# One late weight slot loaded by a half-width transfer and eight transfers of eight partitions, another slot loaded by rows, and the sums of the last but one expert moved behind the last product

## The chip, the cores and the metric

The kernel runs on one core of one Trainium2 chip. The metric is the device time of one execution in microseconds (us), and three runs of the kernel before give 1457.04 us as their median (1456.44 to 1457.23). One more execution was taken by the hardware profiler; all rows below are from that one.

TensorE (PE in the profile) multiplies matrices and writes to PSUM; VectorE (DVE) and ScalarE (ACT) work on whole tiles; SyncE (SP) issues nearly all the transfers from memory. A transfer is carried by sixteen DMA engines.

## The reference

One block over 256 latent tokens and 256 context tokens: modulated norm, an input projection, retention and latent attention, a merge, and then a layer of 32 experts of which each token takes four. The change lies in the experts, whose core is this (cut):

```python
def moe(h, router_w, router_b, w_gu, b_gu, w_down, b_down):
    logits = tok @ router_w + router_b
    top_val, top_idx = lax.top_k(logits, TOP_K)
    gates = jax.nn.softmax(top_val.astype(jnp.float32), axis=-1)
    ...
    def expert_block(args):
        xb, e = args
        gu = xb @ w_gu[e] + b_gu[e]
        gate, up = gu[:, :D_FF_EXPERT], gu[:, D_FF_EXPERT:]
        gate = jnp.minimum(gate, SWIGLU_LIMIT)
        up = jnp.clip(up, -SWIGLU_LIMIT, SWIGLU_LIMIT)
        glu = gate * jax.nn.sigmoid(SWIGLU_ALPHA * gate)
        return ((up + 1.0) * glu) @ w_down[e] + b_down[e]
    ...
    out = jnp.zeros_like(tok).at[sorted_tok].add(ys[dest] * sorted_gate[:, None].astype(ys.dtype))
```

After it come the residual and a last RMSNorm over each token's 1024 columns. All is float32. An expert has 8 MB of weights for gate and up (1024 x 2048) and 4 MB for down (1024 x 1024), so the 32 experts read 384 MB.

## The kernel before

The experts are done one after the other, each for up to 64 tokens. Their weights come in slots of 2 MB: 128 partitions of 16 KB. An expert takes four slots for gate and up (`load_gu`, line 1171) and two for down (`load_down`, line 1176). There are eleven slots in a ring, and the list `todo` sets the order in which they are filled. For experts 0 to 29 it is four gate/up slots, two down slots, and so on. The last two, 30 and 31, stand together: four slots of 30, four of 31, two down slots of 30, two of 31. The last three of these down slots are loaded by `down_in_parts` (line 1184): four transfers of 512 KB, each a quarter of every partition's 16 KB, so that TensorE can begin on a quarter.

SP issues the transfers in order. Besides the slot, a transfer needs a semaphore that counts its landing. There are eight of them (DMAHW0 to DMAHW7 in the lists below), handed out in turn, and an issue waits until the transfer eight places ahead of it has landed on all its engines.

TensorE's order is written by hand. For each expert `gate_up` (matmuls on line 1539) takes four slots of two k each; in its middle `combine` (line 1525) adds the weighted outputs of the expert before to the sums `total`. `slot_rows` (1512, 1514) makes the rows and gates for that. Then `down` (1572) multiplies by the down slots, and `weigh` scales the result (DVE, 1581) and splits it into a high half on ACT (292) and a low half on DVE (293). These halves live in the tiles `up` and `ga` of a pool with one buffer for each name.

At the end this differs. Expert 30's down products are held back. Its hidden rows are made inside expert 31's `gate_up` (`middle`, line 144 transposes, with the final gain on lines 1590 and 1643). After expert 31's `slot_rows` there are sixteen small matmuls on ones that keep TensorE going (`keep_warm`, line 486), as there are for expert 30. Then come expert 30's down products (1572), expert 31's from its first down slot (1723), the sums of expert 30 (1525), expert 31's from its second down slot (1723), the weighing, and expert 31's sums (`add_product`, 1712). What follows is the last norm (1627 to 1738 on ACT and DVE) and four stores.

Of the kernel before, what the change touches and what calls it, by code (L numbers as in the profile page):

```python
# [25 lines left out]
E = 32  # L26
# [33 lines left out]
def hybrid_block(ctx: ExitStack, tc: tile.TileContext, A, out, dbg=None):  # L60
    nc = tc.nc
# [56 lines left out]
    for i, n in enumerate(("ret_decay_fwd", "ret_decay_bwd")):  # L118
        src = A[n]
# [182 lines left out]
    def bank(*names, shape=(128, 512)):  # L302
        for n in names:
            B[n] = pt_(shape)
# [178 lines left out]
    def keep_warm(n):  # L483

        for _ in range(n):
            nc.tensor.matmul(B["spare"][:, :128], ones, ones, start=True, stop=True)
# [682 lines left out]
    def load_gu(wgu, j):  # L1169
        w = wtile()  # L1170
        nc.sync.dma_start(w, wgu[256 * j:256 * j + 256].rearrange("(p r) n -> p (r n)", r=2))
        return w

    def load_down(wdn, j):
        w = wtile()
        nc.sync.dma_start(w, wdn[512 * j:512 * j + 512].rearrange("(p r) n -> p (r n)", r=4))
        return w

    def down_in_parts(wdn, j):
# [3 lines left out]
        for r in range(4):  # L1183
# [4 lines left out]

    todo = [(f, A[name][0, e], i) for es in [[e] for e in range(E - 2)] + [[E - 2, E - 1]]
            for f, name, n in ((load_gu, "exp_w_gu", 4), (load_down, "exp_w_down", 2)) for e in es for i in range(n)]  # L1190
    todo[-3:] = [(down_in_parts, src, i) for f, src, i in todo[-3:]]

    def fetch():
        f, src, i = todo.pop(0)
# [2 lines left out]
    def take(f, src, i):  # L1197

        if src is not None:
            return f(src, i)  # L1200
        if not fetched:
            fetch()
        return fetched.pop(0)
# [3 lines left out]
    def wtile():  # L1207
        r = slots[nring[0] % len(slots)]
        nring[0] += 1
        return r.tile([128, 4096], F32, name="w")  # L1210
# [153 lines left out]
    def one_hot(oh, pos, ne):  # L1364

        shp = [128, 2, ne, CAP]
        nc.vector.tensor_tensor(oh[:, :, :ne], pos[:, :, :, None].to_broadcast(shp),
                                slot[:, None, None, :].to_broadcast(shp), op=OP.is_equal)
# [33 lines left out]
    def row_of(e):  # L1402
        return lambda q: ident[:, 32 * q + e:32 * q + e + 1]
# [38 lines left out]
    def oh_tile():  # L1442
        return late.tile([128, 2, EG, CAP], F32R, name="oh", bufs=2)
# [57 lines left out]
    def xg_tile():  # L1501
        return late.tile([128, 4, EG * CAP], F32, name="xg", bufs=3)

    def slot_rows(oh, i, g, name="ct"):

        ct = late.tile([128, T], F32R, name=name)
        gs = late.tile([128, 1], F32, name=name + "g")
        ps = pt_()
        for t in range(2):
            for h in range(2):  # L1510
                o = oh[:, t, i].bitcast(F32)
                nc.tensor.matmul(ps[64 * h:64 * h + 64, 128 * t:128 * t + 128], o, ident,
                                 start=(t == 0), stop=True, skip_group_check=True)
                nc.tensor.matmul(ps[64 * h:64 * h + 64, T:T + 1], o, g[:, t], start=False, stop=(t == 1),
                                 skip_group_check=True)
        nc.scalar.activation(ct, ps[:, :T], AF.Copy)
        nc.vector.tensor_copy(gs, ps[:, T:T + 1])  # L1517
        return ct, gs

    def combine(ys, ct, n=CAP, first=False):  # L1520

        for t in range(2):
            for part in ys:
                for h in range(2):
                    nc.tensor.matmul(total[t][h], ct[64 * h:64 * h + n, 128 * t:128 * t + 128],  # L1525
                                     part[64 * h:64 * h + n], start=first, stop=(part is ys[-1]), skip_group_check=True)

    def gate_up(wgu, halves, xg, i, mid=None, ga=None):

        sl = slice(CAP * i, CAP * i + CAP)  # L1530
        g_, u_ = halves[0][0], halves[2][0]
        for k in range(KD):
            if mid and k == MID:
                mid()
            if k % 2 == 0:
                w = take(load_gu, wgu, k // 2)
            for ps, h, c in halves:
                c += 2048 * (k % 2)
                nc.tensor.matmul(ps[64 * h:64 * h + 64], xg[k // 4][:, k % 4, sl], w[:, c:c + 512],  # L1539
                                 start=False, stop=(k == KD - 1), skip_group_check=True)  # L1540
        ga = ga() if ga else xp.tile([128, 512], F32, name="ga")
        up = xp.tile([128, 512], F32, name="up")
        nc.vector.tensor_scalar(ga, g_, LIMIT, None, op0=OP.min)  # L1543
        nc.scalar.activation(g_, ga, AF.Tanh, scale=0.5 * ALPHA)  # L1544
        nc.vector.tensor_scalar(up, u_, LIMIT, -LIMIT, op0=OP.min, op1=OP.max)
        nc.vector.scalar_tensor_tensor(up, up, 1.0, ga, op0=OP.add, op1=OP.mult)
        nc.vector.scalar_tensor_tensor(up, g_, 1.0, up, op0=OP.add, op1=OP.mult)
        return up

    def hidden(up, mid=None, hT=None):  # L1550
        ps = pt_((128, 4, 128))

        fours = up.rearrange("s (p r) -> s r p", r=4)
        for c in range(4):
            transpose(ps[:, c], fours[:, c])
        if mid:
            mid()
        hT = hT() if hT else xp.tile([128, 4, 128], F32, name="ga")
        nc.scalar.activation(hT, ps, AF.Copy, scale=0.5)  # L1559
        return [hT[:, f % 4, 64 * (f // 4):64 * (f // 4) + 64] for f in range(KD)]  # L1560
# [39 lines left out]
    for h in range(2):  # L1600
        r = slice(64 * h, 64 * h + E)
# [9 lines left out]
    def gate_rows():  # L1611
        ps = pt_()
        for t in range(2):
            transpose(ps[:, 128 * t:128 * t + 128], gate[:, t].rearrange("p a s -> p (a s)"))
        nc.scalar.activation(gT, ps[:, :T], AF.Copy)
    def add_tokens(t, h):
        hs = slice(512 * h, 512 * h + 512)
        nc.tensor.matmul(total[t][h], ident, x[:, t, hs], start=False, stop=True, skip_group_check=True)
# [19 lines left out]
    def wide():  # L1638

        w = wtile()  # L1640
        fg = [w[:, 2048 + 512 * h:2560 + 512 * h] for h in range(2)]
        for f, ps in zip(fg, final_gain()):
            nc.scalar.activation(f, ps, AF.Copy)
        return w[:, :2048].rearrange("p (t n) -> p t n", t=2), fg
# [7 lines left out]
    pending, before_last = None, {}  # L1652
    for e in range(E):
        g, i = divmod(e, EG)
        last = e == E - 1

        def middle():
            if e == 0:
                gate_rows()
            elif last:  # L1660
                before_last["hT"] = hidden(before_last["up"])
                before_last["out"] = wide()
            else:
                combine(*pending)
        up = gate_up(None, begun.pop(), xg, i, middle, flat if last else None)
        if E - 8 <= e < E - 4:
            add_tokens(*divmod(e - E + 8, 2))
        if e == 0:
            combine((bdn,), gT, E, True)
        ct, gs = slot_rows(oh, i, gt1[:, :, e:e + 1], "ct2" if last else "ct")  # L1670
        if e >= E - 2:
            bank("spare")
            keep_warm(CLK[8])
        if last:
            break
        if i == 0:
            if g + 1 < E // EG:
                ohn = oh_tile()
                one_hot(ohn, posm[:, :, EG * g + EG:EG * g + 2 * EG], EG)
                xgn = []  # L1680
                rbn = slot_scale(ohn, EG)

        def gather_next():
            if g + 1 < E // EG:
                xgn.append(xg_tile())
                gather(ohn, rbn, xgn[i], i, EG)

        if e:
            gather_next()
        if e == E - 2:  # L1690
            before_last.update(up=up, ct=ct, gs=gs)
            begun.append(gu_bias(row_of(e + 1)))
            continue
        ys = down(None, up, gs, lambda: begun.append(gu_bias(row_of(e + 1))))
        pending = (ys, ct)
        if e == 0:
            gather_next()
        if i == EG - 1 and g + 1 < E // EG:
            oh, xg = ohn, xgn
# [4 lines left out]
    ys = down(None, None, before_last["gs"], None, before_last["hT"], lambda: later.append(hidden(up, None, xg_tile)))  # L1704
# [12 lines left out]
    for j in range(2):  # L1717
        w = take(load_down, None, j)
        for f in range(4 * j, 4 * j + 4):
            for c in range(2):  # L1720
                for h in range(2):
                    o = 1024 * (f % 4) + 512 * h + 256 * c
                    nc.tensor.matmul(pys[c][64 * h:64 * h + 64], hT[f], w[:, o:o + 256],  # L1723
                                     start=(f == 0), stop=(f == KD - 1))
        if j == 0:
            combine(ys, before_last["ct"])
    ys = weigh([(slice(256 * c, 256 * c + 256), pys[c]) for c in range(2)], gs)
    for c in range(2):
        add_product(c)
# [75 lines left out]
```

## Time and profile before

| | |
|---|---|
| median of three runs | 1457.04 us |
| profiled execution, own time | 1458.6 us |
| its span | 1456.8 us |
| TensorE busy | 1406.9 us (97%) |
| from about 540 us on: DMA | about 427 GB/s |

Times are in us from the span's start, mean durations of groups in ns. In rows of the timeline, "0.44 PE L1512 ... x4" is a run of four instructions that together took 0.44 us; what follows in brackets is idle time and who ended it. The share of the span in the chain is the work that ended last, followed back from the last instruction. The profiled execution took 1458.6 us, that is 1.8 us above its span and 1.6 us above the median of the runs.

### The profile page before, as it was taken

The numbers are of one execution on the slowest core, as the hardware profiler recorded it, in microseconds if no ns is written. First come the engines' busy times: TensorE is split into PE (matmuls) and PEld (weight loads), VectorE is DVE, ScalarE is ACT, GpSimd is POOL, SyncE is SP. The second block draws the span as 40 slices with busy tenths as digits, with TensorE's granted clock in tenths as the row PEclk, the third lists the DMA queues.
The fourth block names the chain that finished last, engine by engine and source line by source line (L and its number), as shares of the span: only waits on it lengthen the run. The fifth ranks groups of instructions, "written<-read, shape, count | busy, mean of one in ns | idle before, by whom it ended". The sixth has DMA issues, their size and how long they took to land.

```text
span 1456.8 us, 19073 instructions
## 1 busy us (share of the span) xinstructions
PE 1406.9 (97%) x7973; PEld 814.0 (56%) x7973; DVE 561.8 (39%) x1024; ACT 346.5 (24%) x601; POOL 73.1 (5%) x84
## 2 busy tenths in 40 slices
PE   8999999999999999999999999999999899999996
PEld 6788888888888764444434434434433343334333
DVE  4587866868676642221221221221221121212113
ACT  4455633544443421101100100100100010001101
POOL 3200050110101000000000000000000000000000
PEclk9999999999999999999999999999999999999998
DMA  8733283554558889999999999999999999999995
GB/s 280 231 113 130 73 275 101 188 174 163 183 205 318 312 354 413 423 428 426 427 427 427 426 427 426 428 426 427 426 426 428 425 429 425 428 426 426 426 426 197
DMA packets 79284, 492.39 MB, mean 338 GB/s; under 512 B 6819, under 2 KB 25324, under 8 KB 55000
## 3 DMA queue, kind: packets, MB, share of 16 engines
q1 hardware_dynamic: 78216, 489.22, 83.3%
q0 software_dynamic: 576, 1.23, 0.3%
q8 instruction: 64, 1.05, 0.3%
q10 hardware_dynamic: 400, 0.66, 0.1%
q14 instruction: 28, 0.23, 0.0%
HBM read 490.03 MB, written 1.05 MB: 337 GB/s over the span
## 4 chain that ended last, share of the span: by engine, by line
PE 68%; DMA 25%; DVE 4%; ACT 1%; issue 1%; SPq 0%; POOL 0%; DVEq 0%; ACTq 0%; POOLq 0%
PE gu L1539 19%; DMA w<-in_exp_w_gu_dram 16%; PE ps L1572 9%; PE ps L298 9%; PE ps L296 9%; PE ps L297 9%; DMA w<-in_exp_w_down_dram 8%; PE ps L1488 3%; PE gu L1398 3%; PE ps L144 3%; PE sum L1525 2%; DMA w<-in_ada_w_dram 1%; DVE ws L288 1%; PE ps L330 1%; PE gu L1723 0%
## 5 line engine op out<-in xcount | busy, mean ns | idle before, releaser
L1539 PE MATMUL gu<-w,xg 128*64 128x512 f32 x2048 | 455.8, 595 | 17.7 <-DMA w<-in_exp_w_gu_dram 17.2
L1539 PEld LDWEIGHTS gu<-w,xg 128*64 128x64 f32 x2048 | 142.5, 137 | 307.8 <-issue 266.0
L1572 PE MATMUL ps<-w,ga 128*64 128x512 f32 x992 | 218.4, 592 | 0.0
L1543 DVE TENSOR_SCALAR ga<-gu 128x512 f32<-128x512 f32 x31 | 21.4, 692 | 394.9 <-PE gu L1539 394.9
L288 DVE TENSOR_TENSOR ws<-w,ws 128x1024 fp32r<-128x1024 f32 (+1 forms) x114 | 139.6, 1232 | 43.2 <-ACT ws L287 41.4
L1572 PEld LDWEIGHTS ps<-w,ga 128*64 128x64 f32 x992 | 71.1, 137 | 140.7 <-issue 139.3
L287 ACT ACTIVATE ws<-w 128x1024 fp32r<-128x1024 f32 (+1 forms) x114 | 116.7, 1028 | 73.3 <-PE ps L298 71.0
L1544 ACT ACTIVATE gu<-ga 128x512 f32<-128x512 f32 x31 | 18.7, 602 | 433.0 <-DVE ga L1543 433.0
L1581 DVE SCALAR_TENSOR_TENSOR ps<-ps,ctg,gate 128x512 f32<-128x512 f32 x31 | 23.5, 758 | 245.9 <-PE ps L1572 245.9
L296 PE MATMUL ps<-ws,hh 128*128 128x512 f32 (+3 forms) x304 | 111.7, 367 | 1.1 <-ACT hh L408 1.1
L298 PE MATMUL ps<-ws,hl 128*128 128x512 f32 (+3 forms) x304 | 110.0, 362 | 1.2 <-DVE hl L410 1.2
L297 PE MATMUL ps<-ws,hh 128*128 128x512 f32 (+3 forms) x304 | 110.0, 362 | 0.5 <-DVE ws L288 0.5
L292 ACT ACTIVATE up<-ps 128x512 fp32r<-128x512 f32 x31 | 18.5, 597 | 247.8 <-DVE ps L1581 247.8
L1488 PE MATMUL ps<-oh,x 128*128 128x128 f32 x512 | 68.5, 287 | 4.2 <-DVE ctg L1517 4.0
L1488 PEld LDWEIGHTS ps<-oh,x 128*128 128x128 f32 x512 | 62.7, 196 | 7.2 <-DVE ctg L1517 6.2
L296 PEld LDWEIGHTS ps<-ws,hh 128*128 128x128 f32 x304 | 57.5, 189 | 14.9 <-issue 4.2
L298 PEld LDWEIGHTS ps<-ws,hl 128*128 128x128 f32 x304 | 57.6, 190 | 10.6 <-DVE hl L410 2.2
L297 PEld LDWEIGHTS ps<-ws,hh 128*128 128x128 f32 x304 | 57.6, 189 | 9.8 <-DVE ws L288 1.2
L1398 PE MATMUL gu<-bgu,ident 128*64 128x512 f32 x256 | 62.0, 605 | 0.0
L365 DVE SCALAR_TENSOR_TENSOR ada<-w,sc,ada 128x1024 f32<-128x1024 f32 x32 | 40.9, 1278 | 0.0
L1559 ACT ACTIVATE ga<-ps 128x512 f32<-128x512 f32 x31 | 18.5, 597 | 82.6 <-PE ps L144 77.1
L297 PE MATMUL ps<-atl,hth 128*128 128x256 f32 x128 | 35.8, 280 | 0.7 <-DVE atl L293 0.7
(405 smaller groups left out, 1782.7 us busy)
## 6 DMA issues: line engine op xcount, KB each, us to landing
w<-in_exp_w_gu_dram SPq DMA_DIRECT2D x128, 2048.0 KB, 36.4
w<-in_exp_w_down_dram SPq DMA_DIRECT2D x61, 2048.0 KB, 37.9
w<-in_w_in_dram SPq DMA_DIRECT2D x48, 512.0 KB, 4.6
w<-in_ada_w_dram SPq DMA_DIRECT2D x32, 512.0 KB, 6.1
w<-in_ada_w_dram SPq DMA_DIRECT2D x32, 256.0 KB, 6.2
w<-in_w_in_dram SPq DMA_DIRECT2D x32, 256.0 KB, 4.2
w<-in_w_branch_ret_dram SPq DMA_DIRECT2D x16, 512.0 KB, 5.1
w<-in_exp_w_down_dram SPq DMA_DIRECT2D x12, 512.0 KB, 12.2
```

The costliest lines, as they stand in the source:

```text
L144: nc.tensor.transpose(dst, src, ident[:n, :n])
L287: nc.scalar.activation(hi[:, :n], src, AF.Copy)
L288: nc.vector.tensor_tensor(lo[:, :n], src, hi[:, :n].bitcast(F32), op=OP.subtract)
L296: nc.tensor.matmul(ps, a[0], b[0], start=start, stop=False, skip_group_check=True)
L297: nc.tensor.matmul(ps, a[0], b[1], start=False, stop=False, skip_group_check=True)
L298: nc.tensor.matmul(ps, a[1], b[0], start=False, stop=stop, skip_group_check=True)
L365: nc.vector.scalar_tensor_tensor(a, w, sc[:, k:k + 1], a, op0=OP.mult, op1=OP.add)
L1398: nc.tensor.matmul(ps[64 * h:64 * h + 64], pick_row(c // 512).to_broadcast([128, CAP]), bgu, start=True, stop=False, skip_group_check=True)
L1488: nc.tensor.matmul(ps[:, i, :w], pairs(x[:, t], 4)[:, k // 2, k % 2], rhs, start=(t + i == 0), stop=(t == 1), skip_group_check=True)
L1525: nc.tensor.matmul(total[t][h], ct[64 * h:64 * h + n, 128 * t:128 * t + 128], part[64 * h:64 * h + n], start=first, stop=(part is ys[-1]), ...
L1539: nc.tensor.matmul(ps[64 * h:64 * h + 64], xg[k // 4][:, k % 4, sl], w[:, c:c + 512], start=False, stop=(k == KD - 1), skip_group_check=True)
L1572: nc.tensor.matmul(py[64 * h:64 * h + 64], hT[f], w[:, 1024 * r + 512 * h:1024 * r + 512 * h + 512], start=(f == 0), stop=(f == KD - 1))
```

## The change

Four edits, all in the last two experts.

- Expert 31's first gate/up slot (`todo[-8]`) is loaded by `gu_uneven`: one transfer of partitions 0 to 63 (1 MB) and eight of eight partitions (128 KB each), nine transfers where there was one.
- Expert 30's first down slot (`todo[-4]`) is loaded by `down_in_parts` too, so four transfers of 512 KB where there was one of 2 MB.
- After expert 31's `slot_rows` the sixteen small matmuls, and the PSUM bank that they write, are gone (`e == E - 2`).
- The sums of expert 30 (`combine`) come after all products of expert 31, no longer between its two down slots.

```diff
+    def gu_uneven(wgu, j):
+
+        w = wtile()
+        src = wgu[256 * j:256 * j + 256].rearrange("(p r) n -> p (r n)", r=2)
+        for a, b in [(0, 64)] + [(p, p + 8) for p in range(64, 128, 8)]:
+            nc.sync.dma_start(w[a:b], src[a:b])
+        return w
+
...
-    todo[-3:] = [(down_in_parts, src, i) for f, src, i in todo[-3:]]
+    todo[-4:] = [(down_in_parts, src, i) for f, src, i in todo[-4:]]
+    todo[-8] = (gu_uneven, *todo[-8][1:])
...
-        if e >= E - 2:
+        if e == E - 2:
             bank("spare")
             keep_warm(CLK[8])
...
-        if j == 0:
-            combine(ys, before_last["ct"])
+    combine(ys, before_last["ct"])
     ys = weigh([(slice(256 * c, 256 * c + 256), pys[c]) for c in range(2)], gs)
```

The queue of SP near the end, in the kernel before. The first row is expert 30's last gate/up slot; the slots of expert 31 follow; 1587 is the row of the final gain; in brackets is what each issue waits for.

```order
L1171 DMA w<-in_exp_w_gu_dram 128x4096 [waits DMAHW6_49,PE_49]
L1171 DMA w<-in_exp_w_gu_dram 128x4096 [waits DMAHW7_49,PE_49]
L1171 DMA w<-in_exp_w_gu_dram 128x4096 [waits DMAHW0_49,PE_49]
L1587 DMA oh<-in_final_norm_g_dram 8x128 [waits DMAHW1_49,DVE_49,PE_49]
L1171 DMA w<-in_exp_w_gu_dram 128x4096 [waits DMAHW2_49]
L1171 DMA w<-in_exp_w_gu_dram 128x4096 [waits DMAHW3_49]
L1176 DMA w<-in_exp_w_down_dram 128x4096 [waits DMAHW4_49,PE_49]
L1184 DMA w<-in_exp_w_down_dram 128x1024 [waits DMAHW5_49,PE_49]
```

The same place of SP's queue in the changed kernel, from the same slot on (its lines stand eight or nine later; 1179 is `gu_uneven`).

```order
L1171 DMA w<-in_exp_w_gu_dram 128x4096 [waits DMAHW6_49,PE_49]
L1179 DMA w<-in_exp_w_gu_dram 64x4096 [waits DMAHW7_49,PE_49]
L1179 DMA w<-in_exp_w_gu_dram 8x4096 [waits DMAHW0_49]
L1179 DMA w<-in_exp_w_gu_dram 8x4096 [waits DMAHW1_49]
L1179 DMA w<-in_exp_w_gu_dram 8x4096 [waits DMAHW2_49]
L1179 DMA w<-in_exp_w_gu_dram 8x4096 [waits DMAHW3_49]
L1179 DMA w<-in_exp_w_gu_dram 8x4096 [waits DMAHW4_49]
L1179 DMA w<-in_exp_w_gu_dram 8x4096 [waits DMAHW5_49]
L1179 DMA w<-in_exp_w_gu_dram 8x4096 [waits DMAHW6_49]
L1179 DMA w<-in_exp_w_gu_dram 8x4096 [waits DMAHW7_49]
L1171 DMA w<-in_exp_w_gu_dram 128x4096 [waits DMAHW0_49,PE_49]
L1596 DMA oh<-in_final_norm_g_dram 8x128 [waits DMAHW1_49,DVE_49,PE_49]
```

The nine transfers use up all eight semaphores and the first one again: the last piece waits for the half-width transfer, which has DMAHW7 too, and expert 31's second slot for the first piece.

The end of ACT's list in the kernel before, with the tiles' numbers: rows and hidden values of expert 31, then the high half of expert 30's output (`up_9419`) and the first high half of expert 31's (`up_9476`), both in the one buffer of `up`.

```order
L1544 ACTIVATE gu_9282<-xg_9350 128x512 [waits DVE_49]
L1516 ACTIVATE ct2_9357<-ps_9359 128x256 [waits PE_49]
L1559 ACTIVATE xg_9408<-ps_9403 128x512 [waits PE_49]
L292 ACTIVATE up_9419<-ps_9387 128x512 [waits DVE_49]
L292 ACTIVATE up_9476<-gu_9423 128x256 [waits DVE_49,Activation_49]
```

The same rows in the changed kernel.

```order
L1553 ACTIVATE gu_9282<-xg_9358 128x512 [waits DVE_49]
L1525 ACTIVATE ct2_9365<-ps_9367 128x256 [waits PE_49]
L1568 ACTIVATE xg_9402<-ps_9397 128x512 [waits PE_49]
L292 ACTIVATE up_9413<-ps_9378 128x512 [waits DVE_49]
L292 ACTIVATE up_9470<-gu_9417 128x256 [waits DVE_49,PE_49,Activation_49]
```

The last row waits for PE as well: the matmuls that read expert 30's high half now stand after the last products, so its buffer is free only when they have read it. DVE's first low half (line 293) gets the same wait.

## Rows read from the trace of the kernel before

**Rows 1.** The page: share of the chain that ended last, by engine.
```profile
PE 68%; DMA 25%; DVE 4%; ACT 1%; issue 1%; SPq 0%; POOL 0%; DVEq 0%; ACTq 0%; POOLq 0%
```

**Rows 2.** The chain near the end: start us, us, what (x instructions).
```profile
1361.35 39.16 DMA w<-in_exp_w_gu_dram
1400.51 0.04 issue
1400.55 3.65 PE gu L1539 x16
...
1424.94 1.00 PE ps L486 x16
1425.94 3.58 PE ps L1572 x16
...
1437.24 1.12 PE sum L1525 x8
1438.36 3.20 PE gu L1723 x28
1441.56 0.02 issue
1441.58 0.50 DVE gu L1581
```

**Rows 3.** Stretches: us, busy of PE, PEld, DVE, ACT, POOL, PEclk, DMA share, GB/s.
```profile
1385.00:1390.00 5.00, 5.00 (x26) 1.44 (x21) 1.45 (x2) 0.60 (x1) 0.00 (x0) 1.00 0.99 423
1425.00:1430.00 5.00, 5.00 (x36) 2.37 (x34) 1.43 (x4) 0.36 (x1) 0.00 (x0) 1.00 0.92 331
1434.00:1435.00 1.00, 1.00 (x13) 0.66 (x10) 0.59 (x1) 0.37 (x1) 0.00 (x0) 1.00 0.69 254
1435.00:1436.00 1.00, 1.00 (x14) 0.64 (x12) 0.69 (x1) 0.23 (x1) 0.00 (x0) 1.00 0.54 221
1437.00:1438.00 1.00, 1.00 (x12) 0.67 (x8) 0.00 (x0) 0.00 (x0) 0.00 (x0) 1.00 0.52 213
1439.00:1440.00 1.00, 1.00 (x12) 0.71 (x10) 0.00 (x0) 0.00 (x0) 0.00 (x0) 1.00 0.22 90
1440.00:1441.00 1.00, 1.00 (x14) 0.64 (x10) 0.00 (x0) 0.00 (x0) 0.00 (x0) 1.00 0.01 4
```

**Rows 4.** Timeline of SP, single issues: start us, us, engine, line, operation.
```profile
1361.35 0.33 SPq L1171 DMA_DIRECT2D w<-in_exp_w_gu_dram  x1
1366.25 0.33 SPq L1171 DMA_DIRECT2D w<-in_exp_w_gu_dram  x1
1371.16 0.33 SPq L1171 DMA_DIRECT2D w<-in_exp_w_gu_dram  x1
...
1400.52 0.33 SPq L1184 DMA_DIRECT2D w<-in_exp_w_down_dram  x1
1405.42 0.33 SPq L1184 DMA_DIRECT2D w<-in_exp_w_down_dram  x1
1410.34 0.81 SPq L1184 DMA_DIRECT2D w<-in_exp_w_down_dram  x2
...
1425.07 0.33 SPq L1184 DMA_DIRECT2D w<-in_exp_w_down_dram  x1
1430.14 0.33 SPq L1184 DMA_DIRECT2D w<-in_exp_w_down_dram  x1
```

**Rows 5.** Issue to landing: issues at 1366.25 and 1426.35, at 127.27 and 477.61.
```profile
w<-in_exp_w_gu_dram SPq DMA_DIRECT2D x1, 2048.0 KB, 39.2
w<-in_exp_w_down_dram SPq DMA_DIRECT2D x1, 512.0 KB, 10.5
w<-in_mla_w_ukv_dram SPq DMA_DIRECT2D x1, 512.0 KB, 3.6
w<-in_exp_w_gu_dram SPq DMA_DIRECT2D x1, 2048.0 KB, 10.3
```

**Rows 6.** DMA share in tenths, 40 slices of 127 to 131 us; SP's issue there.
```profile
DMA  0000000000001553358999976997766651000000
...
127.27 0.37 SPq L278 DMA_DIRECT2D w<-in_mla_w_ukv_dram  x1
```

**Rows 7.** Timeline of PE and ACT, end: idle before and its releaser in brackets.
```profile
1438.29 3.67 PE L1723 MATMUL gu<-w,xg 128*64 128x256 f32 x32
1442.60 0.39 PE L1712 MATMUL sum<-up,ct 64*128 64x256 f32 x2 [0.64 <-ACT up L292]
...
1442.17 0.76 ACT L292 ACTIVATE up<-gu 128x256 fp32r<-128x256 f32 x2 [6.94 <-DVE gu L1581]
```

## The prediction

> **What bounds the kernel now.** I read the chain of waits first. Over the whole span TensorE holds 68% of it and transfers 25% [rows 1]. Near the end it changes hands once: expert 30's last gate/up slot lands at 1400.51, and from there TensorE's own work runs on to 1441.56 [rows 2]. So anything that TensorE no longer does after 1400 could end the kernel earlier, if the slots it still needs are there.
>
> The second view is the table of stretches, for how far the transfers are behind that. In the steady part DMA is busy throughout at 423 GB/s. At the end the rate doesn't stop at once: from 1434 on it falls to a half (213 GB/s, share 0.52) and stays there until 1438, before it dies out at 1440 [rows 3]. Half of the rate for some 5 us means that about eight of the sixteen engines have finished and the other eight are one slot's time behind. A slot counts as landed only with its last engine, so the lagging half sets every landing.
>
> The third view is SP's queue. Issue 1361.35 landed at 1400.51, and the issue eight places later starts at 1400.52; issue 1366.25 plus its 39.2 is 1405.45, and the next one starts at 1405.42 [rows 2, 4, 5]. So the landing of one transfer is the ticket for the issue eight places on, one ticket per 4.9 us. The last ticket is used at 1430.14; with 10.5 us to land [rows 4, 5] the last quarter of the last slot is there at 1440.7 (the stretch after 1440 moves nothing, rows 3). TensorE takes that quarter as the last fourth of a run that starts at 1438.29 and lasts 3.67 [rows 7], at 1441.04. The slack is 0.3 us: TensorE and the transfers are almost equally late at the end.
>
> **The change part by part.** The sixteen small matmuls go: 1.0 us, from 1424.94 to 1425.94 [rows 2]. Their PSUM bank goes with them; nothing waits for it in rows 2 and 7, so nothing is counted.
>
> The moved sums: eight matmuls, 1.12 us, leave the place before the last slot's products [rows 2]. They land in the gap between the last product and expert 31's own sums, 1441.96 to 1442.60 [rows 7], but they don't fit it. ACT's first high half, at 1442.17, now waits until the buffer of `up` is read, after six of the eight matmuls: 0.84 of 1.12. With a release of about 0.1 that is 0.94 after the last product, where it was 0.21, so 0.7 later; if it waits for all eight, 0.95; if the release is quicker, 0.6. I take 0.7. Behind ACT stand the low half on DVE, all of `add_product` and the whole last norm, so the 0.7 is paid in full. If TensorE were alone, the two edits would give -1.0 - 1.1 + 0.7 = -1.4 us. As the slack is 0.3, what the transfers do decides.
>
> The rows for expert 30's first down slot let TensorE begin it on a quarter; before it was there at 1425.07 [rows 4], 0.9 before its use at 1425.94, and it would be wanted 1.0 earlier. The price is in the transfers: from 1425.07 to 1440.7 twelve quarters took 15.6, 1.30 each, so a slot in quarters is 5.2 against 4.9. I add 0.3; at least 0, if quarters only look slow because half of the engines wait, at most 0.5.
>
> The uneven slot is the large term, and it has two sides. For the bytes: the half-width transfer gives every engine half of a slot's work, 2.45 us, and the eight pieces give the rest to whichever engines carry eight partitions. If those are the leading eight, the lagging half is spared 2.45 us. For the tickets: the nine transfers use nine of them, where one would do. The half-width transfer goes out at 1366.25, the pieces on the tickets on which the kernel before issued 1371.16 and what follows. The seventh gets the one of 1400.52, the eighth waits for the half-width transfer itself, and expert 31's second slot, which had been issued at 1371.16, stands behind it on SP. The half-width transfer ends on the lagging engines at 1400.51 + 2.45 = 1402.96. The eighth piece takes 0.33 [rows 4] and a little, so the second slot is issued at 1403.35, and by then the lagging half has nothing queued.
>
> What such a restart costs is not in this part of the trace. From a near-idle queue the 512 KB issued at 127.27 landed in 3.6 us, its first data 1.0 after the issue [rows 5, 6]. The same bytes in the stream take 1.23 at 427 GB/s, so 2.4 is start and end. The upper end is the 2 MB load at 477.61, which had to share its engines: 10.3 [rows 5], so 5.4 on top of 4.9. The lower end is the 1.0 to first data alone. I take 2.4, since the queue is empty. The second slot then lands at 1403.35 + 2.4 + 4.9 = 1410.65; before it was 1410.34, by the issue that waits for it [rows 4]. So the restart takes back the 2.45 and 0.3 more (from -1.1 to +3.3 by the two ends). After it all engines start together, and the remaining slots follow as before; their tickets come in time, since all nine are back by then.
>
> For which engines carry the pieces, rows 3 show only that there are two halves. The Trainium skill, DMA: Bandwidth & Descriptors, section Why a DMA increments its semaphore by 16 and not by 1, says that a load issued by SP runs on the largest count up to sixteen that divides its slowest dimension, on the lowest-numbered engines. By that the 64 partitions use sixteen and the eight-partition pieces always the same eight; no row numbers the engines. The Trainium skill, DMA: Bandwidth & Descriptors, section Rules for kernel authors, speaks against the change: it advises not to split a transfer by partitions, since the parts share the same engines. By that the time would be the last rival's below; rows 3 only show that the two halves are not equally late.
>
> The sum: the last quarter lands 0.3 + 0.3 = 0.6 later, of which 0.3 is slack, so TensorE's last products start 0.3 later and are not sooner for what it no longer does. With the 0.7 of the moved sums that is +1.0 us. On the profiled execution 1458.6 becomes 1459.6, span 1457.8; for the median of runs, 1457.04 becomes 1458.0.
>
> **The rivals.**
> - Faster: the second slot reaches the lagging half before it runs dry. Then the transfers end 2.45 - 0.3 sooner, at 1438.6; TensorE doesn't wait any more and the -1.4 counts: 1455.6. For it speaks the half-rate tail [rows 3]; against it the order of SP's waits, and that each issue in rows 4 does follow a landing. It can't be more, as from 1400.55 on TensorE has no other idle time to lose.
> - Slower: the pieces fall on the lagging half. Eight pieces are 4.9 us there, from 1402.96 to 1407.9, and the second slot stands behind them: 1412.8 instead of 1410.34. That is 2.45 + 0.3 - 0.3 + 0.7 = +3.2, 1460.2. It decides as soon as those eight engines are the late ones, whatever a restart costs. For it speaks that no row names the half; against it only that one slot is then all the more uneven.
> - Slower by the restart: at the 5.4 of the shared queue it costs 3.0 more, 1461.0. It needs over 4.3 to leave the band of no change. Against it: at 1403 nothing else is queued.
> - The change doesn't do what it says: the pieces run on all sixteen engines. Then there is no shift, each piece is 0.3 on every engine, and they bridge the time to first data (1.0) of the second slot. It lands about when it did, the quarters cost their 0.3, and the sums 0.7, less the slack of 0.3: +0.7, 1457.7.
>
> **How the numbers follow.** My forecast gets 0.58, the evenly spread pieces 0.10, the faster rival 0.13, the pieces on the late half 0.11, the slow restart 0.08. By their conditions, "no change" is within 0.2%, 2.9 us, about what a measurement of this kernel tells: 1454.1 to 1460.0. The faster rival is inside it too, so faster gets 0.03, for something I don't see. The two slower rivals lie at the edge and beyond it: 0.13. Same is 0.84. The likeliest one's own range is 1457.2 to 1459.0; the range for 8 in 10 goes from the faster rival, 1455.5, to the first of the slower ones, 1460.2.
>
> **What would show it.** In the profile after, SP issues expert 31's second slot near 1403.3, not 1371, and the DMA share dips around 1403 to 1405. The half-rate stretch at the end is gone: the rate stays near 400 GB/s until it stops. The last quarter lands near 1441.3. ACT's line 292 is released by PE, 0.9 after the last product. I am wrong if the stretch of half the rate stays or grows (pieces on the late half), if there is no dip and TensorE's last product ends before 1440 (faster), or if the dip lasts over 4 us.

## The result, and the profile after

The changed kernel takes 1471.64 us (median, 1469.47 to 1473.34), the kernel before 1456.84 beside it: a ratio of 1.0093 with a 95% interval of 1.0081 to 1.0105. It is slower by 14.8 us, well outside the range given. Profile against profile it is less: the span is 1467.7 us against 1456.8, so 10.9 us, since the profiled execution of before was a high one and that of after (1469.47 us) the lowest of its runs. The two traces also reach the late part at different times: expert 30's last gate/up slot is issued at 1361.35 before [rows 2] and at 1358.96 after, 2.39 earlier. So a forecast time, which counts on the trace before, stands 2.39 earlier on the trace after; both are given.

The stretches come first (columns as in [rows 3]: us, busy PE, PEld, DVE, ACT, POOL, PEclk, DMA share, GB/s).

```profile
1385.00:1390.00 5.00, 4.06 (x20) 1.20 (x18) 0.86 (x2) 0.60 (x1) 0.00 (x0) 1.00 1.01 429
1390.00:1395.00 5.00, 3.54 (x20) 1.25 (x16) 0.00 (x0) 0.00 (x0) 0.00 (x0) 1.00 1.06 272
1395.00:1400.00 5.00, 3.65 (x16) 1.06 (x16) 0.00 (x0) 0.00 (x0) 0.00 (x0) 1.00 0.89 190
1400.00:1405.00 5.00, 0.14 (x2) 0.14 (x4) 0.00 (x0) 0.00 (x0) 0.00 (x0) 0.98 0.65 157
1405.00:1410.00 5.00, 5.00 (x18) 1.44 (x19) 0.66 (x1) 0.00 (x0) 0.00 (x0) 0.68 0.39 102
1410.00:1415.00 5.00, 4.03 (x44) 2.34 (x43) 2.14 (x5) 0.99 (x2) 0.00 (x0) 1.00 0.99 269
1415.00:1420.00 5.00, 3.70 (x18) 1.24 (x16) 0.00 (x0) 0.00 (x0) 0.00 (x0) 1.00 1.01 427
...
1445.00:1446.00 1.00, 0.80 (x10) 0.28 (x8) 0.00 (x0) 0.00 (x0) 0.00 (x0) 1.00 1.04 414
1446.00:1447.00 1.00, 0.99 (x8) 0.39 (x8) 0.00 (x0) 0.00 (x0) 0.00 (x0) 1.00 1.04 414
1447.00:1448.00 1.00, 0.79 (x8) 0.48 (x8) 0.00 (x0) 0.00 (x0) 0.00 (x0) 1.00 0.31 123
1448.00:1449.00 1.00, 0.84 (x10) 0.41 (x8) 0.00 (x0) 0.00 (x0) 0.00 (x0) 1.00 0.12 49
```

The reader is to look at the last two columns together. From 1390 on the DMA share stays high (1.06, then 0.89) while the rate falls from 429 to 272 and 190 GB/s: the engines are hardly idle, they take longer for the same bytes. Only after 1400 does the share fall far too. From 1390 to 1415 the five stretches move 4.95 MB; at 427 GB/s it would be 10.7, so 13.4 us of transfer time are lost. By what the five shares lack to 1, some 5.4 of them are engines with nothing to move, and some 8 are slow transfers (an estimate). The forecast had a dip of 2.4 us there. At the end the tail at half the rate [rows 3] is gone, as forecast: 414 GB/s until 1447, and then it stops within some 2 us.

Next the queue of SP: the half-width transfer, the fifth to the eighth piece, and expert 31's second slot. Columns as in [rows 4].

```profile
1363.86 0.56 SPq L1179 DMA_DIRECT2D w<-in_exp_w_gu_dram  x1
...
1388.71 0.27 SPq L1179 DMA_DIRECT2D w<-in_exp_w_gu_dram  x1
...
1395.70 0.27 SPq L1179 DMA_DIRECT2D w<-in_exp_w_gu_dram  x1
...
1404.83 0.27 SPq L1179 DMA_DIRECT2D w<-in_exp_w_gu_dram  x1
...
1408.63 0.27 SPq L1179 DMA_DIRECT2D w<-in_exp_w_gu_dram  x1
1409.00 0.35 SPq L1171 DMA_DIRECT2D w<-in_exp_w_gu_dram  x1
```

The waits are those of the forecast, each later. The fifth piece (1388.71) and the sixth (1395.70) wait for the two slots ahead of expert 30's last, the seventh (1404.83) for that slot. The fifth and the seventh are 16.1 us apart, where two tickets were 9.8. The eighth (1408.63) waits for the half-width transfer, which was to land at 1402.96 (on this trace 1400.57). The second slot goes out behind it, at 1409.00 and not near 1403.35 (on this trace 1400.96).

The chain near the end, as in [rows 2]:

```profile
1358.96 45.86 DMA w<-in_exp_w_gu_dram
1404.82 0.04 issue
1404.86 4.46 PE gu L1548 x12
...
1410.19 19.23 DMA w<-in_exp_w_gu_dram
1429.44 11.31 DMA w<-in_exp_w_down_dram
1440.77 10.17 DMA w<-in_exp_w_down_dram
1450.94 0.04 issue
1450.99 1.08 PE gu L1732 x8
1452.07 0.91 PE sum L1534 x6
...
1453.05 0.39 ACT up L292
```

Expert 30's last gate/up slot is a full-width transfer that the change doesn't touch. Before it took 39.16 from issue to landing [rows 2], now 45.86, with the uneven slot's transfers queued behind it. Both the half-width transfer and the pieces can do that, as the experiments show. After it the chain goes from transfer to transfer to the last quarter at 1450.94 (forecast: 1441.3, on this trace 1438.9). The last two rows are the moved sums: six of their matmuls, 0.91, and then ACT's line 292, 0.98 after the last product, as forecast (0.94).

TensorE's products on expert 30's last two slots and expert 31's first two (columns as in [rows 7]):

```profile
1395.73 3.65 PE L1548 MATMUL gu<-w,xg 128*64 128x512 f32 x16 [2.19 <-DMA w<-in_exp_w_gu_dram]
1404.86 5.29 PE L1548 MATMUL gu<-w,xg 128*64 128x512 f32 x16 [5.48 <-DMA w<-in_exp_w_gu_dram]
...
1414.65 3.65 PE L1548 MATMUL gu<-w,xg 128*64 128x512 f32 x16 [0.97 <-DMA w<-in_exp_w_gu_dram]
1419.60 3.65 PE L1548 MATMUL gu<-w,xg 128*64 128x512 f32 x16 [1.30 <-DMA w<-in_exp_w_gu_dram]
```

The wait for expert 30's last slot is 5.48 us, and the sixteen products after it take 5.29 instead of 3.65. The granted clock of their stretch is 0.68: between the two levels, 1.2 and 2.4 GHz, after TensorE had done nothing but wait for most of 1399 to 1405. So the transfers' loss brings 1.6 us on TensorE with it; here the transfers are the later ones and set the end. The uneven slot is there at 1414.6, 6.0 us after its last piece went out, and the second slot at 1419.6, 10.6 us after its issue, where the forecast had 7.3.

### The profile page after: what moved, and what is told of

Read it like the earlier page. It is cut to its first block, busy times and chain, and to the rows that moved or that the text cites. A ratio compares the mean times of both kernels' runs of the same rounds, so it can differ in the third digit from the quotient of the medians.

```text
span 1467.7 us, 19057 instructions
## 1 busy us (share of the span) xinstructions
PE 1408.3 (96%) x7957; PEld 811.1 (55%) x7957; DVE 562.1 (38%) x1024; ACT 346.2 (24%) x601; POOL 73.1 (5%) x84
## 3 DMA queue, kind: packets, MB, share of 16 engines
q8 instruction: 64, 1.05, 0.3%
HBM read 490.03 MB, written 1.05 MB: 335 GB/s over the span
## 4 chain that ended last, share of the span: by engine, by line
PE 62%; DMA 31%; DVE 4%; ACT 1%; issue 1%; SPq 0%; POOL 0%; DVEq 0%; ACTq 0%; POOLq 0%
DMA w<-in_exp_w_gu_dram 23%; PE gu L1548 16%; PE ps L298 9%; PE ps L296 9%; PE ps L297 9%; PE ps L1581 8%; DMA w<-in_exp_w_down_dram 7%; PE ps L1497 3%; PE ps L144 2%; PE gu L1407 2%; PE sum L1534 1%; DMA w<-in_ada_w_dram 1%; DVE ws L288 1%; PE ps L330 1%; DVE up L1554 0%
## 5 line engine op out<-in xcount | busy, mean ns | idle before, releaser
L298 PEld LDWEIGHTS ps<-ws,hl 128*128 128x128 f32 x304 | 57.1, 188 | 10.6 <-DVE hl L410 2.2
```

Of the source, the lines that this page charges most:

```text
L298: nc.tensor.matmul(ps, a[1], b[0], start=False, stop=stop, skip_group_check=True)
```

## Experiments

All stand on one of the two kernels, with the uneven slot's transfers (`todo[-8]`) or some of the edits changed; times are medians of runs, with the kernel before on the same chip. Except where said, the computation is whole.

**Which edit.** Theory: the uneven slot carries the whole loss. Rival: the wait that the moved sums add is dearer than 0.7.

```diff
-    todo[-8] = (gu_uneven, *todo[-8][1:])
```


> The changed kernel without the uneven slot; the other three edits stay. Ports (64 and then eight adjacent partitions are slow to write, and slow all other transfers meanwhile): the whole loss goes, 1456.8 plus 0 to 1 for the sums that now hold up ACT, so 1456.5 to 1457.8. Tickets (nine transfers use up the eight semaphores, the queue runs dry): the same number. Late half (the pieces lie on engines that are behind): the same number. If instead the rows of expert 30's first down slot or the moved sums cost the time, it stays above 1465.

1458.19 beside 1457.58, ratio 1.0006 (0.9996 to 1.0015). The other three edits together are no change. In its profile TensorE waits for each of the last five quarters, of which this is the last; the sums of expert 31 then wait for ACT:

```profile
1438.87 1.08 PE L1731 MATMUL gu<-w,xg 128*64 128x256 f32 x8 [0.17 <-DMA w<-in_exp_w_down_dram]
...
1441.38 0.39 PE L1720 MATMUL sum<-up,ct 64*128 64x256 f32 x2 [0.29 <-ACT up L292]
```

The opposite kernel is the one before with only the new load of that slot:

```diff
+    todo[-8] = (gu_uneven, *todo[-8][1:])
```


> The kernel before with the uneven slot alone. All three theories: the whole loss, 1469 to 1474. Ports: DMA at some 200 GB/s from about 1390 on, with all engines busy.

1471.27, ratio 1.0093 (1.0076 to 1.011). The theory holds: it is the uneven slot alone.

The two edits without the moved sums:

```diff
+        if j == 0:
+            combine(ys, before_last["ct"])
-    combine(ys, before_last["ct"])
```


> The changed kernel without the uneven slot and with expert 30's sums back between the two down slots of expert 31: what is left is the rows for expert 30's first down slot and the sixteen small matmuls taken out. By the prediction's terms, quarters +0.3 on the transfers, slack of 0.3, so no change: 1457.0 to 1457.6 on a kernel before at 1457.0, and 0.7 less than with the sums moved as well (that one measured 1458.19 beside 1457.58). Rival: the moved sums cost nothing, since the transfers set the end and the sums stood in TensorE's wait for them; then this is the same as the kernel with the sums moved, within 0.3. A gain of over 1 us would mean that TensorE alone sets the end.

1458.03 beside 1457.84, ratio 0.9999 (0.9989 to 1.0008). With the sums moved it was 0.61 above its own kernel before, without them 0.19; the intervals overlap, so the 0.7 of the sums is neither shown nor refuted in the times. It is no gain either way.

**Tickets or bytes.** Theory 1: nine transfers on eight semaphores make the stream run dry. Rival: something in what the nine transfers write. First the same nine transfers cut by columns, so that each writes all 128 partitions:

```diff
+        for a, b in [(0, 2048)] + [(c, c + 256) for c in range(2048, 4096, 256)]:
+            nc.sync.dma_start(w[:, a:b], src[:, a:b])
```


> The kernel before with that slot in nine transfers of all 128 partitions: half of the columns, and eight of 256 columns (128 KB). The same bytes and tickets as in the uneven slot, all engines alike, all partitions in each. Ports: only the tickets' bubble is left, 1457 to 1460. Tickets: most of the loss stays, 1466 to 1474. Late half: no loss, 1456.5 to 1458.

1459.47, ratio 1.0016 (1.0007 to 1.0026): 1.9 us, and no more, come with nine transfers on eight semaphores. The issues of the seventh and the eighth piece and of the second slot, on SP:

```profile
1399.43 0.33 SPq L1179 DMA_DIRECT2D w<-in_exp_w_gu_dram  x1
...
1401.97 0.33 SPq L1179 DMA_DIRECT2D w<-in_exp_w_gu_dram  x1
1402.40 0.38 SPq L1171 DMA_DIRECT2D w<-in_exp_w_gu_dram  x1
```

The chain from there, that slot's landing:

```profile
1402.40 8.75 DMA w<-in_exp_w_gu_dram
1411.15 0.02 issue
```

The stretches in the middle and at the end:

```profile
1395.00:1400.00 5.00, 3.77 (x20) 1.12 (x18) 0.00 (x0) 0.00 (x0) 0.00 (x0) 1.00 0.65 260
1400.00:1405.00 5.00, 5.00 (x50) 2.78 (x48) 2.50 (x5) 0.99 (x2) 0.00 (x0) 1.00 0.80 233
...
1438.00:1439.00 1.00, 1.00 (x10) 0.55 (x8) 0.00 (x0) 0.00 (x0) 0.00 (x0) 1.00 1.01 401
1439.00:1440.00 1.00, 1.00 (x12) 0.68 (x10) 0.00 (x0) 0.00 (x0) 0.00 (x0) 1.00 0.54 213
```

This is the course that the prediction drew for the change: the second slot issued when the half of the slot has landed, a dip, no tail at half the rate. Here share and rate fall together from 1395 to 1400 (0.65, and 260 of 427 is 0.61): engines are idle, hardly any is slow. From 1400 to 1405 the rate is lower than the share (0.55 and 0.80), so some transfers, perhaps the pieces with 1 KB of each partition, do take longer; what that adds to the 1.9 isn't parted. The slot lands 8.75 after its issue, where the forecast had 7.3 (2.4 + 4.9); that 1.45 and the 0.3 that it expected anyway make 1.75 of the 1.9. Counted from the landing of expert 30's last slot, for which the seventh piece waits (1399.43; 1400.51 before), the second slot lands 11.7 later and not 9.8: that is the 1.9.

Then the reverse: no tickets to speak of, but two transfers of 64 neighbouring partitions each.

```diff
+        for a, b in [(0, 64), (64, 128)]:
+            nc.sync.dma_start(w[a:b], src[a:b])
```


> The kernel before with that slot in two transfers of 64 partitions, one after the other: every engine has the same bytes, and two tickets are used. Ports: each half is written at half the rate, so the slot costs 2 x 2.4 us and what it slows beside it, 1461 to 1466, with a stretch near 200 GB/s. Tickets: no loss, 1456.5 to 1458. Late half: no loss, 1456.5 to 1458.

1470.02, ratio 1.01 (1.0075 to 1.0125): nearly the whole loss without a single eight-partition piece, and more than the 1461 to 1466 forecast. Its stretches:

```profile
1390.00:1395.00 5.00, 4.78 (x24) 1.73 (x24) 0.00 (x0) 0.00 (x0) 0.00 (x0) 1.00 1.05 295
1395.00:1400.00 5.00, 2.43 (x10) 0.96 (x12) 0.00 (x0) 0.00 (x0) 0.00 (x0) 0.89 1.05 223
1400.00:1405.00 5.00, 2.92 (x8) 0.50 (x5) 0.00 (x0) 0.00 (x0) 0.00 (x0) 0.77 0.98 210
1405.00:1410.00 5.00, 2.60 (x6) 0.77 (x8) 0.00 (x0) 0.00 (x0) 0.00 (x0) 0.57 1.02 223
1410.00:1415.00 5.00, 5.00 (x43) 2.55 (x40) 2.02 (x4) 0.99 (x2) 0.00 (x0) 0.75 0.98 220
1415.00:1420.00 5.00, 4.94 (x27) 1.62 (x26) 0.78 (x3) 0.00 (x0) 0.00 (x0) 1.00 0.97 384
```

With the share at 1.0 throughout, the rate stands at half from 1395 to 1415. In that time 4.4 MB are moved; the slot itself is 2.1. So more than half of the slow bytes belong to slots of full width. Expert 30's last, ahead of it, takes 46.8 from issue to landing.

**Read or written.** Theory: it is the side written, a block of 64 neighbouring partitions in the chip's memory. Rival: the pattern read from memory, or merely that there are two transfers. Three kernels, each with two transfers of 64 partitions; only the places differ. The first writes the even and then the odd partitions, and reads the same; the second writes those, and reads the two halves of the source each in one piece; the third writes halves of 64 neighbouring partitions, and reads every second row pair:

```diff
+        for a, b in [(slice(q, 128, 2), slice(q, 128, 2)) for q in range(2)]:
+            nc.sync.dma_start(w[a], src[b])
...
+        for a, b in [(slice(q, 128, 2), slice(64 * q, 64 * q + 64)) for q in range(2)]:
...
+        for a, b in [(slice(64 * q, 64 * q + 64), slice(q, 128, 2)) for q in range(2)]:
```


> As the two halves of 64 partitions, but the first transfer writes every even partition and the second every odd one (same bytes, same row length, same two tickets; source rows likewise). Write side (a block of 64 adjacent partitions reaches only half of the memory's ways in): the loss is gone, 1456.5 to 1459. Shape (any transfer of 64 partitions is slow): 1468 to 1472, as with the halves.

1457.96 beside 1458.62, ratio 0.9995 (0.9984 to 1.0005): no loss. From 1390 to 1420 its rate is between 419 and 436 GB/s.

> Even and odd partitions written, but from the first and second megabyte of the slot as it lies in memory; the rows of this one slot are thus in other partitions than its use expects, which changes expert 31's values and no instruction. Write side: no loss, 1456.5 to 1459. Read side (two engines reading addresses that are close): the loss stays, 1468 to 1472.

1458.23 beside the same 1458.62, ratio 1.0 (0.9989 to 1.001): no loss. (In this kernel and the next, rows of that slot stand in other partitions, so expert 31 computes other values.)

> Partitions 0 to 63 and 64 to 127 written, but from every second row pair of the slot; again only the place of this slot's rows is another. Write side: the loss stays, 1468 to 1472. Read side: no loss, 1456.5 to 1459.

1471.48 (two runs), ratio 1.0087 (1.0067 to 1.0107): the whole loss. So it is where a transfer writes, and neither of these patterns on the side that is read.

**The pieces.** With the half-width transfer spread over the even partitions, the pieces are left. Theory: eight partitions are slow for the same reason, by where they are. Rival: because few engines carry them. The first kernel takes every sixteenth partition:

```diff
+        for a, b in [(slice(q, 128, n), slice(q, 128, n)) for q, n in [(0, 2)] + [(2 * i + 1, 16) for i in range(8)]]:
+            nc.sync.dma_start(w[a], src[b])
```


> The uneven slot alone, with spread partitions: every second one in the half-width transfer, then eight transfers of eight partitions that lie sixteen apart. Same engines, bytes and tickets as in the uneven slot. Write side: the slow stretch is gone or short; what is left is the tickets' bubble (1.9 with nine column transfers) and whatever the uneven bytes do: 1456 to 1461, below 1459.5 if the late engines are relieved, above if they get more. Shape: 1469 to 1473.

1468.51 (1467.87 to 1469.15) beside 1458.62, so +9.9, ratio 1.0067 (1.005 to 1.0084): far above the 1456 to 1461 of the write side, and just under the other theory's 1469. Its stretches while the pieces run:

```profile
1390.00:1395.00 5.00, 4.08 (x20) 1.52 (x22) 0.00 (x0) 0.00 (x0) 0.00 (x0) 1.00 1.10 393
1395.00:1400.00 5.00, 3.25 (x19) 1.14 (x18) 0.00 (x0) 0.00 (x0) 0.00 (x0) 1.00 0.87 187
1400.00:1405.00 5.00, 1.10 (x6) 0.14 (x2) 0.00 (x0) 0.00 (x0) 0.00 (x0) 1.00 0.73 147
```

From 1390 to 1395 the rate is 393, where the change had 272; then it falls, with more of the share than of the rate left (0.87 at 187). As two transfers over the even and the odd partitions cost nothing, it is the pieces. They too slow slots of full width. The fifth and the seventh piece wait for two such slots, as in the change:

```profile
1390.89 0.56 SPq L1179 DMA_DIRECT2D w<-in_exp_w_gu_dram  x1
...
1406.53 0.56 SPq L1179 DMA_DIRECT2D w<-in_exp_w_gu_dram  x1
```

They are 15.6 us apart, nearly the 16.1 of the change, and not 9.8. Next the same pieces over a wider spread:

```diff
+        for a, b in [(slice(q, b, n), slice(q, b, n)) for q, b, n in [(0, 128, 2)] + [(q, q + 85, 12) for q in range(1, 12, 2)] + [(97, 128, 4), (99, 128, 4)]]:
```


> As the uneven slot of the comb kind (the even partitions in one transfer, then eight transfers of eight odd partitions), but the eight partitions of a piece stand otherwise: six pieces take every twelfth partition, two take every fourth of the upper quarter. Number of transfers, bytes, order and semaphores are the same as where every sixteenth partition was taken, and that kernel took 1468.5 us. Theory 'where it is written': a piece is slow because its eight partitions lie behind few of the ways into the on-chip memory; spread over more of them the pieces no longer slow the stream, the eight-semaphore bubble of 1.9 us (nine column transfers) is left and perhaps a little for pieces on eight engines: 1459 to 1462 us, TensorE's longest wait on expert 31's slots under 3 us. By the Trainium skill, SBUF - State Buffer, section Door 1, pieces of every sixteenth partition reach four of sixteen ports, and these here eight. Rival 'eight engines': a transfer of eight partitions is slow because only eight engines carry it, wherever it is written; then this is 1468 to 1469 us again, with the rate near 150 GB/s from 1395 to 1410.

1464.36 (1463.73 to 1468.17) beside 1457.84, so +6.5, ratio 1.0054 (1.0037 to 1.007). That is between the two: some 3.4 us come back, but not the rest. Both theories missed. Then twice the partitions in each piece, at the same bytes and a like spread:

```diff
+        for q, n, c in [(0, 2, slice(0, 4096))] + [(q, 8, slice(c, c + 2048)) for q in (1, 3, 5, 7) for c in (0, 2048)]:
+            nc.sync.dma_start(w[q::n, c], src[q::n, c])
```


> The even partitions in one transfer, then the odd ones in eight transfers of sixteen partitions and half their columns: every eighth partition, 8 KB of each. Bytes (128 KB), number of transfers, order and semaphores are those of the eight-partition pieces, and a piece lies over as wide a spread of partitions as those that took 1464.36 us; only twice as many partitions take part in a piece. Theory 'engines': what is left of the loss there (6.5 us, of which the eight-semaphore bubble explains 1.9) comes from a piece of eight partitions being carried by eight engines, so that the halves are uneven and the last piece holds back the next slot; with sixteen it is gone: 1458.5 to 1460.5 us, the second slot issued by 1403.5. Rival 'where it is written': only the spread of the partitions counts, and it is the same: 1463 to 1465 us.

1463.96 (1462.53 to 1465.32) beside 1457.71, so +6.25, ratio 1.0047 (1.003 to 1.0064): the same as with eight partitions, as the rival said. Twice the partitions in a piece make no difference to the time. Last, pieces that each lie close together, but neighbours in different places:

```diff
+        for a in [slice(0, 128, 2)] + [slice(q, q + 15, 2) for q in range(1, 128, 16)]:
+            nc.sync.dma_start(w[a], src[a])
```


> The even partitions in one transfer, then eight pieces of eight odd partitions out of sixteen neighbouring ones (1, 3, ... 15, then 17, 19, ... 31 and so on). Every sixteenth partition gave 1468.5 us, every twelfth or fourth 1464.4. Theory 'spread of one piece': each piece by itself lies behind as few ways in as those of every sixteenth partition, so 1467 to 1469.5 us. Rival 'spread of those in flight': neighbouring pieces here take different ways in, where the pieces of every sixteenth partition took the same four in pairs, so what is in flight together covers twice as many: 1463 to 1465.5 us. If it were none of this and the eight engines alone counted, all three would be alike within 1.5 us.

1463.55 (1462.36 to 1465.43), so +5.8, ratio 1.0044 (1.0027 to 1.0061): the rival again. That suggests that what the pieces in flight cover together counts, not each by itself, but doesn't show it. The intervals of these ratios overlap with that of every sixteenth partition, and the last three kernels ran on two other chips; of their twelve runs eleven are below its lowest.

Nine transfers as such (the columns) explain 1.9 of the 5.8 to 6.5 us that are left. Of the other 4 us the traces show a part: slots of full width are still slowed. In the last kernel the fifth and the seventh piece go out 13.1 us apart:

```profile
1388.59 0.62 SPq L1179 DMA_DIRECT2D w<-in_exp_w_gu_dram  x1
...
1401.74 0.62 SPq L1179 DMA_DIRECT2D w<-in_exp_w_gu_dram  x1
```

With every twelfth or fourth partition it is 13.1 as well, with sixteen partitions 12.0, and with pieces that write all 128 partitions 9.8, as two tickets are. So 2.2 to 3.3 of the 4 us are there; what the rest is stays open.

## Why the prediction was wrong

The step that failed is the first sentence on the uneven slot: "the half-width transfer gives every engine half of a slot's work, 2.45 us". It priced a transfer by its bytes over sixteen engines, and put the pieces at 0.61 each in the same way. The price depends on which partitions are written. A block of 64 neighbouring ones runs the whole stream at half the rate, and slots of full width that are in flight beside it too. That term was set at nothing beyond its bytes. By the two halves it is 12.4 us (1470.02 against 1457.58), and by the pieces over every sixteenth partition, with the tickets, 9.9. In the change 13.4 us of transfer time are lost between 1390 and 1415, some 8 of them to slow transfers and the rest to an empty queue.

The Trainium skill has the rule that the prediction should have weighed: SBUF — State Buffer, section Door 1: The DMA port swizzle, says that a transfer's rate depends on how many of sixteen ports into the memory its partitions reach, and that partitions 0 to 63 reach eight of them, as few as 0 to 31, so about 218 GB/s at best. The runs agree: 210 to 223 GB/s with the halves, and no loss with the even and the odd partitions, which by the page's table reach all sixteen. By the same table a piece of every sixteenth partition reaches four ports and each of the wider ones eight: +9.9 and +6.5 us. But a piece out of sixteen neighbouring partitions reaches four by it too, and those cost +5.8, so the ports of one piece alone don't set its price. That neighbours of full width are slowed is this case's own (45.86, and 46.8 with the two halves, against 39.16 us).

Point by point:

- **What bounded the kernel**: right as far as the rows show. In the trace after SP's issues follow the tickets that were named, and the half-rate tail, from which two halves of the engines were inferred, goes once the queue has run empty. No row numbers the engines.
- **Tickets**: right in mechanism, mis-sized. The waits of SP are the ones that were named, and in the kernel with column transfers the second slot is issued 3.0 after expert 30's last slot landed (forecast 2.84, 1403.35 less 1400.51). The restart measured 3.85 there (8.75 less 4.9), inside the bounds of 1.0 to 5.4, where 2.4 was taken. In the change it is 5.7 (10.6 less 4.9), with the last piece still ahead of the slot. The half-width transfer lands at 1408.6, 8.0 later than worked out (on that trace 1400.57), and all behind it moves. One row was misread: the 3.6 us of [rows 5] are those of a like transfer issued at 103.68, as the trace has no landing for the one at 127.27.
- **The lagging half**: the tail at half the rate is gone in the change and with column transfers, as forecast, and stays with two halves (225 and 197 GB/s from 1446 to 1450). The 2.45 that this is worth are already inside the 1.9.
- **The moved sums**: the wait is there in the trace (0.98 after the last product against 0.94 forecast; the bound for all eight matmuls, 0.95 later, is 1.0 by the prediction's own terms). Its cost in the times can't be told from nothing.
- **Matmuls taken out, rows for another slot**: no gain, as forecast. Quarters at the end move 401 to 414 GB/s where whole slots moved 423 [rows 3].
- **The rivals**: none had this. The slow restart came nearest in its sign, but 5.4 of a restart gave 1461.0. The late half, 1460.2, isn't what happened: the tail doesn't stay. The sentence that it would be wrong "if the dip lasts over 4 us" did apply; the dip lasts over 20.
- **Where the time goes**: counted from the issue of expert 30's last slot, expert 31's second slot lands 60.6 us later (1419.6 less 1358.96), before it was 49.0 (1410.34 less 1361.35). Of these 11.6 us, 6.7 are expert 30's last slot (45.86 against 39.16), 1.3 the half-width transfer's end behind it (the second slot goes out 4.18 after that landing, forecast 2.84), 3.3 the longer restart (10.6 against 7.3), and 0.3 were forecast. The last quarter is 12.6 later (1450.94 against 1440.7, and the 2.39 between the traces) and the end of the span 13.3.
- **Not worked out further**: the half-width transfer's share of the loss wasn't parted from the pieces' where both are in blocks: two halves alone cost 12.4, pieces over every sixteenth partition 9.9, and the change with both no more than 14.8, so the two don't add.

## What to carry to other kernels

Price a transfer by the partitions that it writes, not only by its bytes; where a slot has to be cut, cut it by columns, or take every second partition, and leave no block of 64. Read the rate beside the DMA share: here a rate that fell while the share stayed at 1 was slow writes, and one that fell with the share an empty queue. And when a slot is cut into more transfers than there are semaphores (here nine on eight), the next slot's issue comes after the landing of the first part: 1.9 us where every transfer writes all partitions.

## What was not expected of the hardware

- Two transfers of 64 neighbouring partitions, 2 MB in all, hold the stream at 210 to 223 GB/s from 1395 to 1415 at a share of 0.98 to 1.05, full-width transfers included; the same two transfers over even and odd partitions run at 419 to 436.
- The pattern on the side read costs nothing: read as every second 16 KB or in one piece, the even and odd partitions take 1457.96 and 1458.23; the block written with either pattern read, 1470.02 and 1471.48.
- A slot with eight pieces of 128 KB costs by how their partitions lie: +9.9 us for every sixteenth, +5.8 to +6.5 for three other layouts, +1.9 where each piece writes all 128.
- TensorE's granted clock falls to 0.57 in the stretch 1405 to 1410 of the kernel with two halves, in which the engine was busy 2.60 of 5 us after two waits for slots.
